# Moving the small tiles and the 2052-byte tiles of a transformer layer behind all others in SBUF

## The chip, the cores and the metric

The kernel runs on one core of a Trainium2 chip. The metric is the device time of one execution in microseconds (us), the median of several runs. TensorE (PE) multiplies matrices and loads their weights, VectorE (DVE), ScalarE (ACT) and GpSimd (POOL) work elementwise, SyncE (SP) issues the transfers.

## The reference

One layer of a trunk with stick-breaking attention and a SwiGLU feed-forward part, all in float32, for one sequence of 2048 tokens of width 1024, 16 heads of 64 and a feed-forward width of 2816.

```python
mod_all = einsum('bd,lde->lbe', silu(c), ada_w) + ada_b     # shift, scale, gate, twice
h = modulate(rms_norm(x, norm_g[0]), sh_m, sc_m)
q, k, v = split(h @ w_qkv)
sp = where(mask, softplus(z), 0)                            # z = q k / 8, mask: s < t
a = exp(where(mask, z - reverse_cumsum(sp), -inf))
y = (a @ v) @ w_o
x = x + gt_m * rms_norm(y, norm_g[1])
h = modulate(rms_norm(x, norm_g[2]), sh_f, sc_f)
y = (silu(h @ w_g) * (h @ w_u)) @ w_out
x = x + gt_f * rms_norm(y, norm_g[3])
```

## The kernel before

Every float32 product is made of three matmuls (`mm3`, L148 to L150) of a high and a low half of each operand: high by high, high by low, low by high. A matmul has 128 rows of weights (128x128) and as a rule 512 columns of the moving operand. The instructions of TensorE, ScalarE, VectorE and GpSimd are issued in the order in which the program writes them.

The work comes in these parts, by the names of their tiles:

- The attention loop, to about 1400 us. A slot of the loop handles one 128x512 block of scores: `z` (L507, two matmuls, weights `qt`, moving `kt`), two sigmoids (ScalarE, L524 and L526), a scan (VectorE, L536 or L541, into `w`), a product (GpSimd, L548, into `a`), transposes of `a` (L558, four for a block in full, moving the identity in `begin`, into `t`), a split of the transposed tile into `aT` (L568 ScalarE, L574 VectorE), and the product with the values (`o`, L586, two matmuls, weights `v`, moving `aT`). A list written out by hand, `ORDER_IN_SLOT`, sets the order in a slot: in every second slot two tiles are transposed. Between them stand the matmuls of the projections (`pj`, moving `ht`, weights `w` in tag whl) that make the queries, keys and values of later blocks.
- The output projection (`y`, weights `ohl`, moving `wo`), with transposes `h2T` (L899) between its matmuls, to about 1580 us.
- The up projection of the feed-forward part (`s`, weights `l`, moving `r`), to about 2450 us: 44 groups of 7 products with 4 steps each, 84 matmuls a group. Both factors are made by seven products instead of eight.
- The down projection (`o`, moving `b`, weights `ol_qt` and `ol_aT`): 56 accumulations of 11 steps, 8 of them with weights in `ol_qt` and 3 in `ol_aT`.

The tiles lie in one pool, `att`. A tile has a tag, a tag has as many buffers as `BUFS` says, and the pool places the tags one behind the other in the order in which they are first used. What counts below is where a tile begins in its partition, modulo 512 bytes (its residue; a weight slice of 128 float32 is 512 bytes, a moving row of 512 is 2048, so the residue is the same for every slice of a tile). The built program has them at these places:

| tags (bytes of one buffer) | what TensorE reads from them | residue before |
|---|---|---|
| `begin` (2052) | the identity for transposes, which starts 1536 bytes in | 128 |
| `ones` (512) | a few narrow sums | 160 |
| v, qt, wraw, qkn, ht, a, kt (2048 to 8192) | `v`, `qt`, `kt`, `ht`, `a`, `r` in ten of 14 steps, `l`, `b`, `ol_qt`, `ohl`, `wo` in part | 64 |
| ten, four and four tiles of 4 bytes (`rms_ssq`, `rms_ms`, `rms_rstd`) | nothing | |
| w (3 of 2052) | a few early tiles | 128, 160, 192 |
| whl (8192) | weights of the projections, `r` in the last four of 14 steps, `wo` in part | 224 |
| `sc` (32) | nothing | |
| tmp, aT (2048, 4096) | `aT`, `ol_aT`, values before their transposes | 256 |
| 18 tiles of 4 bytes (`carry`, `rms_ms2`) | nothing | |

A tile of 4 bytes takes up 32, one of 2052 takes up 2080. The steps of `r` go by `RIGHT_TAGS`:

```python
RIGHT_TAGS = [
    ("kt", "kt"), ("kt", "v"), ("v", "v"), ("qt",), ("qt",), ("qt",),
    ("kt", "kt"), ("kt", "kt"), ("v", "v"), ("v", "v"),
    ("whl",), ("whl",), ("whl",), ("whl",),
]
```

Each of the 14 serves two steps, six matmuls, so a group has 60 matmuls with `r` at 64 and then 24 with `r` at 224. In the output projection, `wo_load` puts three of the first half's four pairs in whl and all others in ht.

Of the kernel before, what the change touches and what calls it, by code (L numbers as in the profile page):

```python
# [76 lines left out]

def f32(ap):
    return ap.bitcast(F32)
# [3 lines left out]
def hybrid_trunk_kernel(  # L83
# [25 lines left out]
    ones = const.tile([P, P], F32, name="ones")  # L109
    nc.vector.memset(ones, 1.0)  # L110
# [7 lines left out]
    gc = const.tile([P, 2, KC], F32, name="gc")  # L118
    gate_rows = dram.tile([2, P, D], F32, name="gate_rows")
# [16 lines left out]
    def rms_scale(pool, src, tag, junk):  # L136

        ssq = pool.tile([P, 1], F32, name=f"{tag}_ssq", tag="rms_ssq", bufs=10)
        nc.scalar.activation(junk, src, AF.Square, accum_out=ssq)
        ms = pool.tile([P, 1], F32, name=f"{tag}_ms", tag="rms_ms", bufs=4)  # L140
        nc.vector.tensor_scalar(ms, ssq, 1.0 / D, EPS, op0=ALU.mult, op1=ALU.add)
        rstd = pool.tile([P, 1], F32, name=f"{tag}_rstd", tag="rms_rstd", bufs=4)
        nc.gpsimd.tensor_tensor(rstd, ms, mhalf, op=ALU.pow)
        return rstd
# [8 lines left out]
    att = ctx.enter_context(tc.tile_pool(name="att", bufs=2))  # L153
    zps = ctx.enter_context(tc.tile_pool(name="zps", bufs=3, space=PSUM))
# [7 lines left out]

    weights, keys, values, queries = {}, {}, {}, {}
# [3 lines left out]
    def load_weights(p, t, tag="wraw"):  # L167
        raw = att.tile([P, KC, P], F32, name=f"wr{p}_{t}", tag=tag, bufs=BUFS[tag])
        nc.sync.dma_start(raw, wqkv[p, t])
        raws[p, t] = raw  # L170

    def split_weights(p, t):
        raw = raws.pop((p, t))
        hl = att.tile([P, 2, KC, P], F32R, name=f"w{p}_{t}", tag="whl", bufs=BUFS["whl"])
        nc.scalar.copy(hl[:, 0], raw)
        nc.gpsimd.tensor_tensor(hl[:, 1], raw, f32(hl[:, 0]), op=ALU.subtract)
        weights[p, t] = hl[:, 0], hl[:, 1]

    def split_early(p, t, tags):

        raw = raws.pop((p, t))
        if len(tags) == 1:
            hl = att.tile([P, 2, KC, P], F32R, name=f"w{p}_{t}", tag=tags[0], bufs=BUFS[tags[0]])
            hi, lo = hl[:, 0], hl[:, 1]
        else:
            hi, lo = [
                att.tile([P, KC, P], F32R, name=f"w{p}_{t}_{j}", tag=tag, bufs=BUFS[tag])
# [7 lines left out]
    def ada_load(seg, half, k0, n, tag, bufs):  # L195
        w = att.tile([P, n, BT], F32, name=f"aw{seg}_{half}_{k0}", tag=tag, bufs=bufs)
        nc.sync.dma_start(w, ada_w[seg - 2, half, :, k0 : k0 + n])
        return w
# [19 lines left out]
    def ada_done(seg, ps, which, ks=slice(0, KC)):  # L218
# [6 lines left out]
        sc = att.tile([P, KC], F32, name=f"sc{which}_{ks.start}", tag="sc", bufs=1)[:, ks]  # L225
# [5 lines left out]
    def late_modulation(segs, tag, n, ahead, waits, pool, ptag, acc_tag="tmp", rows_tag="wraw", settle=3, pace=1):  # L231
# [10 lines left out]
        for at, (seg, half, k0) in enumerate(chunks):  # L242
# [5 lines left out]
            if k0 == 0:  # L248
                acc = att.tile([P, BT], F32, name=f"aacc{seg}_{half}", tag=acc_tag, bufs=BUFS[acc_tag])
# [11 lines left out]
            if seg in (2, 5):  # L261
                g = seg // 3
                rows = att.tile([P, 2, BT], F32, name=f"gr{g}_{half}", tag=rows_tag, bufs=BUFS[rows_tag])
# [17 lines left out]
    def x_load(b):  # L281
        for i in range(4):
            r0 = b * BT + i * P
            xt = att.tile([P, D], F32, name=f"x{b}_{i}", tag="v", bufs=BUFS["v"])
# [3 lines left out]
    def x_square(b, i):  # L288
        xn = att.tile([P, D], F32, name=f"xn{b}_{i}", tag="kt", bufs=BUFS["kt"])
        x_norm[b, i] = xn  # L290
        x_rstd[b, i] = rms_scale(att, x_tiles[b, i], f"n0_{b}_{i}", junk=xn)
# [16 lines left out]
    def modulate(hl, pt, which, k, name, how="aap"):  # L308

        full = att.tile([P, BT], F32, name=name, tag="tmp", bufs=BUFS["tmp"])  # L310
# [12 lines left out]
    def h_load(p, b):  # L323
        h = []
        for k2 in range(KC // 2):
            ht = att.tile([P, 2, 2, BT], F32R, name=f"ht{p}_{b}_{k2}", tag="ht", bufs=BUFS["ht"])
# [6 lines left out]
    def first_norm(b, k):  # L333
        if b is None or k >= KC:
            return
        if k % 2 == 0:
            ht = att.tile([P, 2, 2, BT], F32R, name=f"ht0_{b}_{k // 2}", tag="ht", bufs=BUFS["ht"])
# [8 lines left out]
    def unpark():  # L346
        p, b = PARKED
        kt = att.tile([P, 2, BT], F32R, name=f"kt{p}_{b}", tag="kt", bufs=BUFS["kt"])
# [5 lines left out]
        qt = att.tile([P, 2, 2, BT], F32R, name=f"qt{p}_{b}", tag="qt", bufs=BUFS["qt"])  # L354
# [5 lines left out]
        v = att.tile([P, 4, 2, 2, HD], F32R, name=f"v{p}_{b}", tag="v", bufs=BUFS["v"])  # L360
# [3 lines left out]
    def project(at):  # L364
# [43 lines left out]
        def split(acc, tag):  # L408
            hl = att.tile([P, 2, BT], F32R, name=f"{tag}n{p}_{b}", tag="qkn", bufs=BUFS["qkn"])
# [13 lines left out]
        else:  # L423
            kt = att.tile([P, 2, BT], F32R, name=f"kt{p}_{b}", tag="kt", bufs=BUFS["kt"])
# [12 lines left out]
        else:  # L437
            qt = att.tile([P, 2, 2, BT], F32R, name=f"qt{p}_{b}", tag="qt", bufs=BUFS["qt"])
# [9 lines left out]
        vT = att.tile([P, BT], F32, name=f"vT{p}_{b}", tag=tag, bufs=BUFS[tag])  # L448
        nc.scalar.copy(vT, acc)

        def values_turn():
# [6 lines left out]
            v = att.tile([P, 4, 2, 2, HD], F32R, name=f"v{p}_{b}", tag="v", bufs=BUFS["v"])  # L458
# [54 lines left out]
    def sigmoids(i, r):  # L513
# [4 lines left out]
        rest = att.tile([P, BT + 1], F32, name=f"w{i}_{r}", tag="w", bufs=BUFS["w"])  # L518
        a = att.tile([P, BT], F32, name=f"a{i}_{r}", tag="a", bufs=BUFS["a"])
# [9 lines left out]
    def break_sticks(i, r):  # L529
# [15 lines left out]
        if sc > 0:  # L545
            carries[r] = att.tile([P, 1], F32, name=f"c{i}_{r}", tag="carry", bufs=10)
# [16 lines left out]
    def split_high(i, j):  # L563
# [3 lines left out]
        hl = att.tile([P, 2, BT], F32R, name=f"aT{i}_{j}", tag="aT", bufs=BUFS["aT"])  # L567
# [10 lines left out]
    def weigh_values(i, j):  # L578
# [11 lines left out]
        if sc == 0 and j == 3:  # L590
            o = att.tile([P, BT], F32, name=f"os{p}_{e}_{qb}", tag="tmp", bufs=BUFS["tmp"])
# [12 lines left out]
    def ada_chunk(q, kh):  # L604
        ks = range(KC // 2 * kh, KC // 2 * (kh + 1))
        if q == 2:
            for k in ks:
                w = att.tile([P, 2, AQ], F32, name=f"ac{q}_{k}", tag="a", bufs=BUFS["a"])
# [4 lines left out]
        w = att.tile([P, 2, KC // 2, AQ], F32, name=f"ac{q}_{kh}", tag=tag, bufs=BUFS[tag])  # L613
# [8 lines left out]
    def ada_sum(q, k):  # L622
        w, scale = chunks[q, k], c_act[:, k : k + 1]
        if q not in piece_sums:
            acc = att.tile([P, 2, AQ], F32, name=f"asum{q}", tag="w", bufs=BUFS["w"])
# [26 lines left out]
    def ada_cols_done(q):  # L652
# [3 lines left out]
        sc = att.tile([P, KC], F32, name=f"sc0_{q}", tag="sc", bufs=1)[:, :2]  # L656
# [9 lines left out]
    def weights_high(t):  # L666
        hl = att.tile([P, 2, KC, P], F32R, name=f"w0_{t}", tag="whl", bufs=BUFS["whl"])
# [15 lines left out]
    def full_high(m):  # L683
        if m % 2 == 0:
            ht = att.tile([P, 2, 2, BT], F32R, name=f"ht0_0_{m // 2}", tag="ht", bufs=BUFS["ht"])
            first_h.extend([ht[:, 0], ht[:, 1]])
            norm_tile[0] = ht
        full = att.tile([P, BT], F32, name=f"hf0_{m}", tag="tmp", bufs=BUFS["tmp"])
# [138 lines left out]
    def mean_square(ssq, tag):  # L827

        ms = att.tile([P, 1], F32, name=f"{tag}_ms", tag="rms_ms", bufs=4)
        nc.vector.tensor_scalar(ms, ssq[0], 1.0 / D, EPS, op0=ALU.mult, op1=ALU.add)  # L830
        ms2 = att.tile([P, 1], F32, name=f"{tag}_ms2", tag="rms_ms2", bufs=4)
        nc.vector.scalar_tensor_tensor(ms2, ssq[1], 1.0 / D, ms, op0=ALU.mult, op1=ALU.add)
        rstd = att.tile([P, 1], F32, name=f"{tag}_rstd", tag="rms_rstd", bufs=4)
# [3 lines left out]
    def sum_squares(src, tag):  # L837
        junk = att.tile([P, BT], F32, name=f"{tag}_junk", tag="tmp", bufs=BUFS["tmp"])
        ssq = att.tile([P, 1], F32, name=f"{tag}_ssq", tag="rms_ssq", bufs=10)
# [6 lines left out]
    def x1_load(b, i):  # L846
        r0 = b * BT + i * P
        xt = att.tile([P, D], F32, name=f"xr{b}_{i}", tag="aT", bufs=BUFS["aT"])
# [3 lines left out]
    def y_square(b, i, half):  # L852
        acc = y_ps.pop((b, i, half))
        y_ssq[b, i, half] = sum_squares(acc, f"y{b}_{i}_{half}")
        if (b, half) == (0, 0):

            if i % 2 == 0:
                y_held[i] = att.tile([P, 2, BT], F32, name=f"yh{i}", tag="wraw", bufs=BUFS["wraw"])
            t = y_held[i - i % 2][:, i % 2]
            nc.vector.tensor_copy(t, acc)  # L860
        else:
            t = att.tile([P, BT], F32, name=f"yt{b}_{i}_{half}", tag="a", bufs=BUFS["a"])
# [25 lines left out]
    def x1_scale(b, i):  # L888
        rstd, x1 = y_rstd.pop((b, i)), x1_tiles.pop((b, i))
        for half, sl in enumerate(HALVES):  # L890
            n = att.tile([P, BT], F32, name=f"x1n{b}_{i}_{half}", tag="a", bufs=BUFS["a"])
# [3 lines left out]
    def h2_turn(b, k):  # L895
# [6 lines left out]
        full = att.tile([P, BT], F32, name=f"h2f{b}_{k}", tag="tmp", bufs=BUFS["tmp"])  # L902
# [7 lines left out]
    def o_load(b, k):  # L910
        tag = "qt" if b else "wraw"
        parts = att.tile([P, 2, BT], F32, name=f"op{b}_{k}", tag=tag, bufs=BUFS[tag])
# [5 lines left out]
    def o_add(b, k):  # L918
        parts = o_parts.pop((b, k))
        o = att.tile([P, BT], F32, name=f"of{b}_{k}", tag="tmp", bufs=BUFS["tmp"])  # L920
# [4 lines left out]
    def o_prep(b, k):  # L925
        o = o_sum.pop((b, k))
        tag = O_TAGS[b % 2][k]
        hl = att.tile([P, 2, BT], F32R, name=f"ohl{b}_{k}", tag=tag, bufs=BUFS[tag])
# [6 lines left out]
    def split_wo():  # L935

        for half, sl in enumerate(HALVES):
            for k in range(KC):
                raw = att.tile([P, BT], F32, name=f"wor{half}_{k}", tag="tmp", bufs=BUFS["tmp"])
# [3 lines left out]
                hl = att.tile([P, 2, BT], F32R, name=f"wos{half}_{k}", tag="qkn", bufs=BUFS["qkn"])  # L943
# [6 lines left out]
    def wo_load(half, k2, tag):  # L950
        hl = att.tile([P, 2, 2, BT], F32R, name=f"wo{half}_{k2}", tag=tag, bufs=BUFS[tag])
# [14 lines left out]
    def gate_load(which, tiles):  # L966
        for half, sl in enumerate(HALVES):
            tiles.append(att.tile([P, BT], F32, name=f"gate{which}_{half}", tag="w", bufs=BUFS["w"]))
# [140 lines left out]
    def sums_load(s, kt):  # L1109

        if s == 0:
            tag = "qt" if kt < 3 else "whl"
            t = att.tile([P, 4, BT], F32, name=f"ts{s}_{kt}", tag=tag, bufs=BUFS[tag])
# [8 lines left out]
        for j in range(2):  # L1122
            t = att.tile([P, 2, BT], F32, name=f"ts{s}_{kt}_{j}", tag="aT", bufs=BUFS["aT"])
# [24 lines left out]
    def right_alloc(s, m):  # L1148
        tags = RIGHT_TAGS[m]
        if len(tags) == 2:  # L1150
            right_parts[s, m] = [
                att.tile([P, 2, BT], F32R, name=f"r{s}_{m}_{j}", tag=t, bufs=BUFS[t])
                for j, t in enumerate(tags)
            ]
        else:
            t = att.tile([P, 2, 2, BT], F32R, name=f"r{s}_{m}", tag=tags[0], bufs=BUFS[tags[0]])
# [22 lines left out]
    def left_load(n):  # L1179
        for t, tag in enumerate(("wraw", "qkn")):  # L1180
            raw = att.tile([P, KC, P], F32, name=f"wi{n}_{t}", tag=tag, bufs=BUFS[tag])
# [3 lines left out]
    def left_add(n, product):  # L1185
# [9 lines left out]
        t = att.tile([P, H4, P], F32, name=f"ls{n}_{product}", tag="tmp", bufs=BUFS["tmp"])  # L1195
# [3 lines left out]
    def left_split(n, product):  # L1199
# [3 lines left out]
        if j == 0:  # L1203
            tag = "whl" if (n, pair) == (0, 0) else "ht"
            left_pair[n, pair] = att.tile(
# [25 lines left out]
    def a_load(m):  # L1231
# [3 lines left out]
            att.tile([P, 2, n, P], F32R, name=f"ol{m}_{t}", tag=t, bufs=BUFS[t])  # L1235
# [15 lines left out]
    def b_load(at, g, which):  # L1251
        par, half = block(which)
        raw = att.tile([P, BT], F32, name=f"br{at}_{g}", tag="a", bufs=BUFS["a"])
# [3 lines left out]
    def chain_tile(version, g):  # L1257

        if g < 8 and g % 2 == 0:
            tag = ("wraw", "qkn")[g // 2 % 2]  # L1260
            t = att.tile([P, 2, BT], F32, name=f"ch{version}_{g}", tag=tag, bufs=BUFS[tag])
            chain[g], chain[g + 1] = t[:, 0], t[:, 1]
        elif g >= 8:
            chain[g] = att.tile([P, BT], F32, name=f"ch{version}_{g}", tag="tmp", bufs=BUFS["tmp"])
# [12 lines left out]
    def b_split(at, g):  # L1277
        src = out_raw.pop((at, g)) if OUT_PRODUCTS[at] in (1, 2) else chain[g]
        tag = "kt" if (at * GO + g) % 14 < 7 else "v"
        hl = att.tile([P, 2, BT], F32R, name=f"b{at}_{g}", tag=tag, bufs=BUFS[tag])  # L1280
# [13 lines left out]
    def keep(src, name, tag):  # L1294
        t = att.tile([P, BT], F32, name=name, tag=tag, bufs=BUFS[tag])
# [296 lines left out]
```

## Time and profile before

| | |
|---|---|
| median of 3 runs | 2877.15 us (2875.82 to 2877.48) |
| profiled execution | 2873.52 us, of which the span of its instructions 2871.1 us |
| TensorE matmuls | 13848, busy 98% of the span |
| VectorE, ScalarE, GpSimd busy | 71%, 57%, 45% |
| transfers | 516.84 MB, mean 180 GB/s |

A row of the timeline gives the start and the drawn length of an instruction, its engine, line, operation and tiles. Matmuls overlap: the drawn length of one reaches into the next, and it is the distance of the starts that says how long TensorE spends on each.

### The profile page before, as it was taken

The page shows a single profiled execution, that of the slowest core. Times are in us where ns is not written, and L with a number is a line of the kernel's source. Part 1 is how long each engine was busy: PE and PEld are TensorE (multiplying, and loading weights), DVE is VectorE, ACT ScalarE, POOL GpSimd, SP SyncE. Part 2 cuts the span into 40 slices and gives each one's busy share as a digit, 9 for nine tenths or more (in the row PEclk, how much of TensorE's full clock was granted, in tenths as well). Part 3 has the DMA queues.
Part 4 walks back from the last instruction along what each step waited for, and adds up shares of the span by engine and source line. Part 5 has one row for each costly group of instructions (what it writes and reads, how often), then busy time and mean ns, then how long its engine had stood idle before and what let it go on. Part 6 is the DMA issues. An engine that isn't in the chain of part 4 may idle for free.

```text
span 2871.1 us, 41790 instructions
## 1 busy us (share of the span) xinstructions
PE 2818.2 (98%) x13848; PEld 2335.4 (81%) x13848; DVE 2027.7 (71%) x2821; ACT 1634.5 (57%) x3265; POOL 1280.4 (45%) x2032
## 2 busy tenths in 40 slices
PE   7999999999999999999999999999999999999998
PEld 6788888888888888887888788888778888888887
DVE  6788888888888888888866666555776655134377
ACT  5787777787777877778645533334433333322243
POOL 1465666576576655666410122221222222544454
PEclk9999999999999999999999999999999999999999
DMA  8765546656665635546389544334453335545575
GB/s 324 270 210 165 187 156 223 209 174 227 191 210 184 216 113 175 191 133 227 97 292 313 193 136 151 121 92 163 130 165 118 111 93 175 190 132 153 181 226 186
DMA packets 239367, 516.84 MB, mean 180 GB/s; under 512 B 22320, under 2 KB 110384, under 8 KB 221488
## 3 DMA queue, kind: packets, MB, share of 16 engines
q1 hardware_dynamic: 239152, 514.18, 55.2%
q8 instruction: 109, 1.79, 0.3%
q14 instruction: 106, 0.87, 0.1%
HBM read 346.85 MB, written 118.49 MB: 162 GB/s over the span
## 4 chain that ended last, share of the span: by engine, by line
PE 88%; DVE 5%; DMA 3%; ACT 2%; issue 1%; POOL 0%; SPq 0%; DVEq 0%; POOLq 0%; ACTq 0%
PE s L148 9%; PE s L149 9%; PE s L150 9%; PE o L586 8%; PE z L507 8%; PE t L558 8%; PE pj L148 6%; PE pj L149 6%; PE pj L150 6%; PE o L149 5%; PE o L148 5%; PE o L150 4%; PE y L148 1%; PE y L150 1%; PE y L149 1%
## 5 line engine op out<-in xcount | busy, mean ns | idle before, releaser
L548 POOL TENSOR_TENSOR a<-a,w 128x512 f32<-128x512 f32 (+3 forms) x640 | 620.5, 969 | 221.7 <-DVE w L541 131.7
L541 DVE TENSOR_TENSOR_SCAN w<-z,c,begin 128x512 f32<-128x512 f32 x384 | 489.8, 1279 | 87.1 <-ACT z L526 68.3
L148 PE MATMUL s<-r,l 128*128 128x512 f32 x1232 | 484.5, 393 | 7.0 <-DVE p L1352 4.5
L149 PE MATMUL s<-r,l 128*128 128x512 f32 x1232 | 482.0, 391 | 0.0
L150 PE MATMUL s<-r,l 128*128 128x512 f32 x1232 | 481.8, 391 | 0.0
L524 ACT ACTIVATE a<-z 128x512 f32<-128x512 f32 (+3 forms) x640 | 347.5, 543 | 171.8 <-PE z L507 140.8
L586 PE MATMUL o<-aT,v 128*128 128x512 f32 (+3 forms) x1280 | 387.5, 384 | 0.1
L574 DVE TENSOR_TENSOR aT<-t,aT 128x512 fp32r<-128x512 f32 (+3 forms) x640 | 359.4, 595 | 23.7 <-ACT aT L568 23.2
L507 PE MATMUL z<-kt,qt 128*128 128x512 f32 (+3 forms) x1280 | 363.5, 365 | 0.0
L568 ACT CAST aT<-t 128x512 fp32r<-128x512 f32 (+3 forms) x640 | 314.2, 534 | 75.7 <-PE t L558 65.5
L526 ACT ACTIVATE z<-z 128x512 f32<-128x512 f32 (+3 forms) x640 | 345.1, 539 | 0.0
L1360 POOL TENSOR_TENSOR one<-p,p 128x512 f32<-128x512 f32 x44 | 71.1, 1616 | 595.3 <-issue 307.6
L148 PE MATMUL pj<-ht,w 128*128 128x512 f32 x768 | 312.7, 407 | 7.6 <-ACT ht L693 2.6
L149 PE MATMUL pj<-ht,w 128*128 128x512 f32 x768 | 305.3, 398 | 1.2 <-DVE ht L698 0.7
L558 PEld LDWEIGHTS t<-begin,a 128*128 128x128 f32 x2176 | 255.7, 141 | 58.5 <-DVE aT L574 10.3
L150 PE MATMUL pj<-ht,w 128*128 128x512 f32 x768 | 302.8, 394 | 0.0
L558 PE MATMUL t<-begin,a 128*128 128x128 f32 x2176 | 294.7, 273 | 7.9 <-DVE aT L574 6.8
L148 PEld LDWEIGHTS s<-r,l 128*128 128x128 f32 x1232 | 231.5, 188 | 60.2 <-DVE p L1352 6.3
L150 PEld LDWEIGHTS s<-r,l 128*128 128x128 f32 x1232 | 231.5, 188 | 50.8
L149 PEld LDWEIGHTS s<-r,l 128*128 128x128 f32 x1232 | 231.6, 188 | 50.2 <-issue 0.5
L507 PEld LDWEIGHTS z<-kt,qt 128*128 128x128 f32 x1280 | 230.5, 188 | 40.1
L536 DVE TENSOR_TENSOR_SCAN w<-z,begin 128x128 f32<-128x128 f32 (+3 forms) x256 | 208.7, 818 | 76.4 <-ACT z L526 66.6
(159 smaller groups left out, 4868.1 us busy)
## 6 DMA issues: line engine op xcount, KB each, us to landing
ht<-h_s SPq DMA_DIRECT2D x108, 1024.0 KB, 8.2
wi<-in_win SPq DMA_DIRECT2D x86, 512.0 KB, 4.1
qt<-qn SPq DMA_DIRECT2D x124, 256.0 KB, 4.7
ol_qt<-act_s SPq DMA_DIRECT2D x56, 512.0 KB, 3.7
act_s<-S SPq DMA_DIRECT2D x66, 256.0 KB, 4.2
br<-in_wout SPq DMA_DIRECT2D x66, 256.0 KB, 3.5
h_s<-ht SPq DMA_DIRECT2D x16, 1024.0 KB, 7.8
o_s<-os SPq DMA_DIRECT2D x128, 128.0 KB, 2.4
```

The source lines that it names most:

```text
L148: nc.tensor.matmul(acc, lhs[0], rhs[0], start=first, stop=False, **kw)
L149: nc.tensor.matmul(acc, lhs[0], rhs[1], start=False, stop=False, **kw)
L150: nc.tensor.matmul(acc, lhs[1], rhs[0], start=False, stop=last, **kw)
L507: nc.tensor.matmul(z[:, :n], q[:, e, part, r * P : (r + 1) * P], k[:, e, :n], start=part == 0, stop=part == 1,)
L524: nc.scalar.activation(a[:, :n], z[:, :n], AF.Sigmoid, scale=QK_SCALE)
L526: nc.scalar.activation(z[:, :n], z[:, :n], AF.Sigmoid, scale=-QK_SCALE)
L541: nc.vector.tensor_tensor_scan(rest[:, rev], left[:, rev], begin[:, :BT][:, rev], initial=carries[r], op0=ALU.mult, op1=ALU.bypass,)
L548: nc.gpsimd.tensor_tensor(a[:, :n], a[:, :n], rest[:, 1 : n + 1], op=ALU.mult)
L558: nc.tensor.transpose(pt[:, rb * P : (rb + 1) * P], weighed[i, rb][:, j * P : (j + 1) * P], ident)
L568: nc.scalar.copy(hl[:, 0, t0:], pt[:, t0:])
L574: nc.vector.tensor_tensor(hl[:, 1, t0:], pt[:, t0:], f32(hl[:, 0, t0:]), op=ALU.subtract)
L586: nc.tensor.matmul(acc[:, t0:], lhs, hl[:, part, t0:], start=sc == qb and j == 0 and part == 0, stop=sc == 0 and j == 3 and part == 1,)
```

## The change

A second pool, `odd`, is opened behind `att` in SBUF, and the tags whose buffers are not whole multiples of 512 bytes go there. All other tiles stay in `att`, in the same order. `ones` moves behind the other constants, and a tile `fill` of 64 bytes is put behind it; it is filled once and read by nothing. All else in the program stays, instruction by instruction, but for the places in SBUF.

```diff
+ODD_TAGS = ("rms_ssq", "rms_ms", "rms_ms2", "rms_rstd", "carry", "sc", "w")
...
-    ones = const.tile([P, P], F32, name="ones")
-    nc.vector.memset(ones, 1.0)
     mhalf = const.tile([P, 1], F32, name="mhalf")
     nc.vector.memset(mhalf, -0.5)
...
     gc = const.tile([P, 2, KC], F32, name="gc")
+
+    ones = const.tile([P, P], F32, name="ones")
+    nc.vector.memset(ones, 1.0)
+    fill = const.tile([P, 16], F32, name="fill")
+    nc.vector.memset(fill, 0.0)
...
     att = ctx.enter_context(tc.tile_pool(name="att", bufs=2))
+    odd = ctx.enter_context(tc.tile_pool(name="odd", bufs=1))
...
+    def sb(shape, dtype, **kw):
+        return (odd if kw["tag"] in ODD_TAGS else att).tile(shape, dtype, **kw)
...
-        raw = att.tile([P, KC, P], F32, name=f"wr{p}_{t}", tag=tag, bufs=BUFS[tag])
+        raw = sb([P, KC, P], F32, name=f"wr{p}_{t}", tag=tag, bufs=BUFS[tag])
```

The last pair of lines stands for all others: each `att.tile` becomes `sb`. The places afterwards:

| tags | residue after |
|---|---|
| `begin` | 128 |
| `ones` | 64 |
| v, qt, wraw, qkn, ht, a, kt, whl, tmp, aT | 128 |
| w | 192, 224, 256 |

More of the change, by code (lines that the diff above doesn't have):

```diff
@@ L224, in ada_done @@
             return
-        sc = att.tile([P, KC], F32, name=f"sc{which}_{ks.start}", tag="sc", bufs=1)[:, ks]
+        sc = sb([P, KC], F32, name=f"sc{which}_{ks.start}", tag="sc", bufs=1)[:, ks]
         nc.vector.tensor_tensor(sc, ps, b_cols[:, 2 * which + 1, ks], op=ALU.add)
@@ L901, in h2_turn @@
             )
-        full = att.tile([P, BT], F32, name=f"h2f{b}_{k}", tag="tmp", bufs=BUFS["tmp"])
+        full = sb([P, BT], F32, name=f"h2f{b}_{k}", tag="tmp", bufs=BUFS["tmp"])
         nc.scalar.activation(
```

142 lines of the change are left out of this document (71 added, 71 removed).

## The prediction

> **What bounds the kernel now.** I read the page's busy times first, then the chain of waits, then the timeline of TensorE, because the first two say that nothing else needs to be read for the end of this kernel.
>
> ```profile
> PE 2818.2 (98%) x13848; PEld 2335.4 (81%) x13848; DVE 2027.7 (71%) x2821; ACT 1634.5 (57%) x3265; POOL 1280.4 (45%) x2032
> PEclk9999999999999999999999999999999999999999
> PE 88%; DVE 5%; DMA 3%; ACT 2%; issue 1%; POOL 0%; SPq 0%; DVEq 0%; POOLq 0%; ACTq 0%
> ```
>
> TensorE is busy for 98% of the span at full clock, and 88% of the chain that ended last is TensorE's own work, so what it spends on each matmul is the kernel's time. The busy column can't give that price: each 128x512 matmul is drawn about 390 ns long and overlaps the next one. The distance from one start to the next is the price. It can be read off the timeline of TensorE (columns: start in us, drawn length, engine, line, operation, tiles, count), between two rows whose number of matmuls in between is known.
>
> The first stretch lies in the up projection of the feed-forward part (tile `s`). A group there is 84 matmuls of 512 columns: 60 whose moving tile `r` has the tags kt, v and qt, at residue 64, then 24 whose `r` has the tag whl, at residue 224. The weights `l` are at 64 in all of them. At 1697.91 the 60 end and the 24 begin.
>
> ```profile
> 1690.43 0.39 PE L148 MATMUL s<-r,l 128*128 128x512 f32 x1
> ...
> 1697.91 0.40 PE L148 MATMUL s<-r,l 128*128 128x512 f32 x1
> ...
> 1703.53 0.40 PE L148 MATMUL s<-r,l 128*128 128x512 f32 x1
> ```
>
> Same line, same engines beside it, same weights: 33 matmuls in 7.48 us are 226.7 ns each, and the next 24 in 5.62 us are 234.2 ns each. What changed is the residue of the moving tile. That difference, 7.5 ns, is the subject of this prediction.
>
> The second stretch is in the down projection (tile `o` with `b`): nine matmuls whose weights `ol_aT` are at 256 from 2500.17 on, then fifteen whose weights `ol_qt` are at 64 from 2502.23 on, all with the moving tile at 64.
>
> ```profile
> 2500.17 0.39 PE L148 MATMUL o<-b,ol_aT 128*128 128x512 f32 x1
> ...
> 2502.23 0.39 PE L148 MATMUL o<-b,ol_qt 128*128 128x512 f32 x1
> ...
> 2505.63 0.39 PE L148 MATMUL o<-b,ol_qt 128*128 128x512 f32 x1
> ```
>
> 2.06 us over 9 are 228.9 ns, 3.40 us over 15 are 226.7 ns. So it matters on the weights' side too, and the cheap value returns when both operands stand at one residue.
>
> The third stretch is the attention loop, which mixes projections `pj` (moving ht at 64, weights whl at 224), scores `z` (64 and 64), value products `o` (moving aT at 256, weights 64) and transposes `t` (moving begin at 128, weights `a` at 64).
>
> ```profile
> 712.79 1.04 PE L558 MATMUL t<-begin,a 128*128 128x128 f32 x8
> 713.59 0.70 PE L586 MATMUL o<-aT,v 128*128 128x512 f32 x2
> 714.13 0.62 PE L507 MATMUL z<-kt,qt 128*128 128x512 f32 x2
> ...
> 717.63 0.60 PE L558 MATMUL t<-begin,a 128*128 128x128 f32 x4
> ```
>
> From 714.13 to 717.63 there are 15 matmuls of 512 columns (four z, two o, nine pj): 233.3 ns each, 6.6 above the cheap value, and the z among them pay although both their operands are at 64. The order of the stream matters, then, not only the matmul itself.
>
> The fourth stretch shows how long. In the output projection (tile `y`) four transposes at 128 and 64 are followed by matmuls with both operands at 64: once nine, once twenty-four.
>
> ```profile
> 1453.80 0.40 PE L149 MATMUL y<-wo,ohl 128*128 128x512 f32 x1
> ...
> 1455.67 0.60 PE L899 MATMUL h2T<-begin,x1n 128*128 128x128 f32 x4
> ...
> 1466.49 0.39 PE L149 MATMUL y<-wo,ohl 128*128 128x512 f32 x1
> ...
> 1467.88 0.39 PE L149 MATMUL y<-wo,ohl 128*128 128x512 f32 x1
> ...
> 1471.73 0.40 PE L148 MATMUL y<-wo,ohl 128*128 128x512 f32 x1
> ```
>
> The first eight of the nine (after the one that directly follows the transposes) take 1.87 us, 233.8 ns each. Of the twenty-four, six take 1.39 us (231.7 ns each), and the next 17 take 3.85 us (226.5 ns each). A stream at one residue thus falls into the cheap step, but only after some six matmuls, and something at another residue throws it out again.
>
> **The change part by part.** It moves addresses. The order of the instructions on all five engines, their shapes and what they wait for stay as they are, but for three fills on VectorE. Afterwards every large tile that TensorE reads is at 128, and so is the identity in `begin`; only `w` (a few early reads) and `ones` (a few narrow matmuls) are elsewhere. How many matmuls each class has is read from the groups by line and shape:
>
> ```profile
> L148 PE MATMUL s<-r,l 128*128 128x512 f32 x1232 | 484.5, 393 | 7.0 <-DVE p L1352 4.5 <-ACT p L1296 2.4
> L148 PE MATMUL pj<-ht,w 128*128 128x512 f32 x768 | 312.7, 407 | 7.6 <-ACT ht L693 2.6 <-DVE qn L411 1.4 <-issue 1.4
> L586 PE MATMUL o<-aT,v 128*128 128x512 f32 x896 | 302.0, 418 | 0.1
> L558 PE MATMUL t<-begin,a 128*128 128x128 f32 x2176 | 294.7, 273 | 7.9 <-DVE aT L574 6.8 <-POOL w L176 0.5
> L507 PE MATMUL z<-kt,qt 128*128 128x512 f32 x896 | 282.5, 396 | 0.0
> L148 PE MATMUL y<-wo,ohl 128*128 128x512 f32 x256 | 104.0, 406 | 0.0
> L149 PE MATMUL o<-b,ol_aT 128*128 128x512 f32 x168 | 66.2, 394 | 0.0
> L148 PE MATMUL o<-b,ol_qt 128*128 128x512 f32 x448 | 174.3, 389 | 0.0
> ...
> L574 DVE TENSOR_TENSOR aT<-t,aT 128x512 fp32r<-128x512 f32 (+3 forms) x640 | 359.4, 595 | 23.7 <-ACT aT L568 23.2
> ```
>
> *Up projection.* 3 x 1232 = 3696 matmuls, 24 in 84 of them at 224: 1056. They lose 7.5 ns each: 7.9 us. No transposes come between, so I take this whole.
>
> *Down projection.* 3 x 168 = 504 matmuls with `ol_aT`, 2.2 ns each: 1.1 us.
>
> *Attention loop.* 3 x 768 pj, 896 z and 896 o make 4096 matmuls of 512 columns. Those directly behind transposes (713.59 to 714.13 holds two o in 0.54 us, so one of them is longer for another reason) and those that wait for another engine I leave out, one in nine: 3640 are left. At 6.6 ns each there are 24.0 us to be had if the cheap step holds always. But transposes still come, and I can't see from this trace whether eight transposes at 128 and 128 keep the step. I take it that they don't, and that six matmuls behind each run of them still pay 5.0 ns (231.7 less 226.7). L574 splits each turned tile once, so there are 640 of them; the order written out for a slot puts two in a run, which makes 320 runs with 4096 / 320 = 12.8 matmuls each, one of which directly follows. Six of 11.8 paying 5.0 of 6.6 ns keep 39% of the loss; 61% of 24.0 us is 14.6 us.
>
> *Output projection.* 3 x 256 = 768 matmuls. Three of the eight weight tiles have the tag whl, so 288 matmuls have the moving tile at 224, and at some 7 ns they are worth 2.0 us. Transposes come between in part of it, so I take 1.3; the bounds are 0.5 and 2.8 (a further 0.8 for the nine at 1453.80 and their like).
>
> *Transposes.* 2176 in the loop, and some 400 elsewhere. In the run at 712.79, eight reach to the next start in 0.80 us, a little over 0.1 us each. No row has a transpose with both operands at one residue. The nearest rows are those of the `s` stretch, where equal residues take 3% off a step; I bound a transpose by the same 3% either way, 3.3 ns, which over 2176 is plus or minus 7 us. I take zero, because no row gives the sign.
>
> *The fills.* `ones` moves behind `mhalf`, and a fill of 128x16 is new.
>
> ```profile
> 0.83 0.17 DVE L110 MEMSET ones<- 128x128 f32 x1 [0.83 <-PEq L1579]
> 0.95 0.06 DVE L112 MEMSET mhalf<- 128x1 f32 x1
> 1.01 0.06 DVE L620 MEMSET acol<- 128x4 f32 x1
> 6.45 0.15 DVE L141 TENSOR_SCALAR n_ms<-n_ssq 128x1 f32<-128x1 f32 x1 [5.38 <-ACT xn L139]
> ```
>
> VectorE then sits idle for 5.38 us, which hides 0.06 to 0.17 us; without that cover it would cost just that.
>
> *The other engines.* Their tiles move too. The scan that writes `w` has three buffers at three residues (128, 160, 192) already:
>
> ```profile
> L541 DVE TENSOR_TENSOR_SCAN w<-z,c,begin x384: 1251/1282/1286, 122.1 to 1403.9; 128x512 f32<-128x512 f32 x192
> ```
>
> Shortest, median and longest lie within 3%, so VectorE does not care; I take zero for it, ScalarE and GpSimd.
>
> *What is late next.* In the middle of the attention loop:
>
> ```profile
> 400.00:1200.00 800.00, 792.56 (x4340) 667.26 (x4338) 684.07 (x891) 626.15 (x1318) 509.55 (x1046) 1.00 0.58 189
> ```
>
> The columns after the length are TensorE, its weight loads, VectorE, ScalarE and GpSimd. VectorE is busy 684 of 800 us. If TensorE's part shrinks by 2%, VectorE goes from 86% to 87%; it stays behind, but some waits grow (the transposes wait 6.8 us in all for aT, above). I bound what is given back between nothing and a fifth of the loop's 14.6 us, 2.9, and take 1.5.
>
> Sum: 7.9 + 1.1 + 14.6 + 1.3 - 1.5 = 23.4 us. The profiled execution took 2873.5 us, 3.6 below the median of 2877.15; a saving of this kind is the same in each, so 2877.15 - 23.4 = 2853.8 us (2850.1 for an execution like the profiled one).
>
> A rule speaks against the change. The Trainium skill, "TensorE: Matmul & The Clock Gate", section "Step-by-step: what each phase is for", says that TensorE has two independent read ports and that "Loading the next tile's weights doesn't steal SBUF read bandwidth from the running matmul". By that rule where the two operands lie would not matter and the sum would be zero; the 226.7 against 234.2 ns above, in one line, disagree.
>
> **The rivals.** *The step holds through the transposes too.* Then the whole 24.0 us of the loop come, and 2.0 of the output projection: 7.9 + 1.1 + 24.0 + 2.0, less a tenth of the loop's, 2.4, given back, is 32.6: 2844.5 us. For it: all tiles then have one distance. Against: the step of a transpose isn't that of a matmul, and order mattered even among matmuls at 64.
>
> *Transposes throw it out for good.* For it: the nine at 1453.80 never settled. The loop then keeps all its loss and only 7.9 + 1.1 + 0.5 = 9.5 us come: 2867.7 us.
>
> *Nothing moves.* The slower step would come from something else that the whl tiles have, such as being written by GpSimd or read in another order; 2877 us. Against: in the `s` stretch r is loaded by the same queue and written by ScalarE and VectorE whatever its tag. The rule quoted above would also give this time.
>
> *Slower: the cheap step belongs to residue 64, not to equality.* Every equal pair in this trace stands at 64, none at 128. If a tile at 128 pays what one at 224 pays, those now cheap go from 226.7 to 234.2: 2640 `s`, 1344 of the down projection with `ol_qt` (its groups have 448 in each of three lines) and some 480 `y`, 4464 x 7.5 = 33 us, against nothing gained: 2910 us. It decides in the `s` stretch: above 230 ns per matmul with r in kt, it is this. For it: no row excludes it. Against: with weights at 256 and the moving tile at 64, the price is 228.9, neither 226.7 nor 234.2, so it goes with the pair.
>
> **How the numbers follow.** The forecast has 0.50, the step that holds throughout 0.21, the loop that keeps its loss 0.14, nothing 0.06, slower 0.09. The first three are faster by over 0.2% (5.8 us, about what a measurement of this kernel can tell from no change): 0.85; the same 0.06; slower 0.09. The predicted time is the likeliest, 2853.8 us. The range leaves out the slower case and no change, and about a twentieth beyond the gains. Below, it reaches past 2844.5 by most of the transposes' 7 us: 2838. Above, it takes in 2867.7 and a little of their cost: 2870.
>
> **What would show it.** In the profile after: the `s` stretch at 226.7 ns through all 84 matmuls of a group; the nine `ol_aT` at 226.7; in the attention loop, matmuls that fall from 233 to 226.7 some way behind each run of transposes, or all at once; transposes still at 0.11 us; waits of TensorE in the loop a little longer. I am wrong if an `s` with r in kt takes over 230 ns, if the loop's 233 ns stays, or if VectorE's scan takes more than its 1282 ns.

## The result, and the profile after

| | before | changed |
|---|---|---|
| median of 6 runs each | 2875.9 us (2871.06 to 2877.48) | 2856.2 us (2853.0 to 2860.04) |
| profiled execution | 2873.52 us | 2853.0 us |
| its span | 2871.1 us | 2851.0 us |

The ratio of the times is 0.9933, with a 95% interval of 0.992 to 0.9946: faster by 19.7 us in the median and by 20.1 in the span of the two profiled executions. The prediction said 23.4. The changed kernel's page, in the lines that the prediction showed first (busy times, granted clock, shares of the chain that ended last):

```profile
PE 2798.8 (98%) x13848; PEld 2336.3 (82%) x13848; DVE 2021.7 (71%) x2822; ACT 1631.8 (57%) x3265; POOL 1276.4 (45%) x2032
PEclk9999999999999999999999999999999999999999
PE 87%; DVE 5%; ACT 3%; issue 2%; DMA 2%; POOL 1%; SPq 0%; DVEq 0%; POOLq 0%; ACTq 0%
```

TensorE has as many matmuls as before and the same share of a shorter span; its idle time went from 2871.1 - 2818.2 = 52.9 to 2851.0 - 2798.8 = 52.2 us. So the 20 us came out of what a matmul costs, and not out of waits. The timeline of TensorE says where. Line numbers are 7 higher in `mm3`, now L155 to L157, and 12 higher in what follows it.

The up projection, one group of 84 matmuls: its start, its 61st matmul (the first with `r` in whl) and the 85th.

```profile
1956.94 0.39 PE L155 MATMUL s<-r,l 128*128 128x512 f32 x1
...
1970.54 0.39 PE L155 MATMUL s<-r,l 128*128 128x512 f32 x1
...
1975.98 0.39 PE L155 MATMUL s<-r,l 128*128 128x512 f32 x1
```

60 in 13.60 us are 226.7 ns each, and the 24 with `r` in whl take 5.44 us, 226.7 ns each, where they took 234.2 before. The down projection, with weights in `ol_qt` from 2482.71 and in `ol_aT` from 2488.15 on:

```profile
2482.71 0.39 PE L155 MATMUL o<-b,ol_qt 128*128 128x512 f32 x1
...
2488.15 0.39 PE L155 MATMUL o<-b,ol_aT 128*128 128x512 f32 x1
...
2489.96 0.39 PE L157 MATMUL o<-b,ol_aT 128*128 128x512 f32 x1
```

24 in 5.44 us are 226.7 ns each, and the eight steps behind `ol_aT` take 1.81, 226.3 each (228.9 before). The attention loop, behind a run of eight transposes:

```profile
712.87 1.03 PE L570 MATMUL t<-begin,a 128*128 128x128 f32 x8
713.66 0.71 PE L598 MATMUL o<-aT,v 128*128 128x512 f32 x2
714.21 0.62 PE L519 MATMUL z<-kt,qt 128*128 128x512 f32 x2
714.66 0.39 PE L155 MATMUL pj<-ht,w 128*128 128x512 f32 x1
...
716.02 0.62 PE L598 MATMUL o<-aT,v 128*128 128x512 f32 x2
716.48 0.33 PE L519 MATMUL z<-kt,qt 128*128 128x128 f32 x2
```

From 714.21 to 716.48 are ten matmuls in 2.27 us, 227.0 ns each; the same kind of stretch took 233.3 before. Behind the transposes the stream has to settle, that is, to come back to the cheap step of 226.7 ns. In the output projection, behind four transposes, that takes longer:

```profile
1453.84 0.39 PE L156 MATMUL y<-wo,ohl 128*128 128x512 f32 x1
...
1455.68 0.60 PE L911 MATMUL h2T<-begin,x1n 128*128 128x128 f32 x4
1456.04 0.48 PE L155 MATMUL y<-wo,ohl 128*128 128x512 f32 x1
1456.35 0.40 PE L156 MATMUL y<-wo,ohl 128*128 128x512 f32 x1
...
1458.44 0.39 PE L156 MATMUL y<-wo,ohl 128*128 128x512 f32 x1
...
1459.80 0.39 PE L156 MATMUL y<-wo,ohl 128*128 128x512 f32 x1
```

The first matmul behind the transposes, at 1456.04, takes 0.31 us. From 1456.35 on nine in 2.09 us are 232.2 ns each, and then six in 1.36 are 226.7. Step by step the nine take 235, 233, 236, 224, 231, 236, 228, 233 and 231 ns. The eight from 1453.84 to the transposes, which took 233.8 ns each before, take 230.0: they settle in part before the next transposes come.

These are samples. The sum over all is made from the starts of all 13848 matmuls: for each of 512 columns the step to the next start less 226.67 ns (for 384 and 256 columns less 170.0 and 113.3); steps that are over 20 ns longer are waits and are counted apart.

| excess over the cheap step, us | before | changed | gained |
|---|---|---|---|
| up projection, `s` | 8.51 | 0.57 | 7.9 |
| down projection, `ol_aT` | 1.17 | 0.00 | 1.2 |
| loop, `pj` | 13.69 | 6.67 | 7.0 |
| loop, `z` | 5.69 | 5.20 | 0.5 |
| loop, `o` | 4.72 | 2.18 | 2.5 |
| output projection, `y` | 2.83 | 1.15 | 1.7 |
| all (with `ol_qt`, about 0) | 36.60 | 15.78 | 20.8 |

### The profile page after: what moved, and what is told of

Its sections match the earlier page's. It is cut to its first block, busy times and chain, and to the rows that moved or that the text cites. A ratio compares the mean times of both kernels' runs of the same rounds, so it can differ in the third digit from the quotient of the medians.

```text
span 2851.0 us, 41791 instructions
## 1 busy us (share of the span) xinstructions
PE 2798.8 (98%) x13848; PEld 2336.3 (82%) x13848; DVE 2021.7 (71%) x2822; ACT 1631.8 (57%) x3265; POOL 1276.4 (45%) x2032
## 4 chain that ended last, share of the span: by engine, by line
PE 87%; DVE 5%; ACT 3%; issue 2%; DMA 2%; POOL 1%; SPq 0%; DVEq 0%; POOLq 0%; ACTq 0%
PE s L155 9%; PE s L157 9%; PE s L156 9%; PE z L519 8%; PE o L598 8%; PE t L570 8%; PE pj L155 6%; PE pj L156 6%; PE pj L157 6%; PE o L157 4%; PE o L156 4%; PE o L155 4%; PE y L157 2%; PE y L155 2%; PE y L156 2%
## 5 line engine op out<-in xcount | busy, mean ns | idle before, releaser
L155 PE MATMUL s<-r,l 128*128 128x512 f32 x1232 | 482.9, 392 | 5.9 <-DVE p L1364 3.5
L157 PE MATMUL s<-r,l 128*128 128x512 f32 x1232 | 480.5, 390 | 0.0
L155 PE MATMUL pj<-ht,w 128*128 128x512 f32 x768 | 310.0, 404 | 7.6 <-ACT ht L705 2.6
L157 PE MATMUL pj<-ht,w 128*128 128x512 f32 x768 | 302.5, 394 | 0.0
L155 PEld LDWEIGHTS s<-r,l 128*128 128x128 f32 x1232 | 231.7, 188 | 56.7 <-DVE p L1364 5.2
L157 PEld LDWEIGHTS s<-r,l 128*128 128x128 f32 x1232 | 231.8, 188 | 48.4
L156 PEld LDWEIGHTS s<-r,l 128*128 128x128 f32 x1232 | 231.8, 188 | 48.1 <-issue 0.5
```

The costliest lines, as they stand in the source:

```text
L155: nc.tensor.matmul(acc, lhs[0], rhs[0], start=first, stop=False, **kw)
L156: nc.tensor.matmul(acc, lhs[0], rhs[1], start=False, stop=False, **kw)
L157: nc.tensor.matmul(acc, lhs[1], rhs[0], start=False, stop=last, **kw)
```

## The experiments

Two things had to be told apart from what the prediction says: whether it is the *distance* between the two operands that counts (theory 1), or where a tile stands by itself, modulo 64 or 256 bytes say (theory 2); and what throws the stream out of the cheap step, the identity's place or the transposes as such. All edits are made on the changed kernel, whose tiles stand at 128. In the lists below a distance is that of the weights less that of the moving tile, modulo 256.

**All tiles 32 bytes further.** A tile of 32 bytes ahead of all others puts every residue from 128 to 160.

```diff
+    lead = const.tile([P, 8], F32, name="lead")
+    nc.vector.memset(lead, 0.0)
     begin = ...
```

> A tile of 32 bytes ahead of all others puts every tile that TensorE reads at residue 160 instead of 128, the identity too; all distances stay. If the price of a matmul goes by the distance of the two operands (theory 1), nothing changes: 2856 us, the up projection at 226.7 ns a matmul with r in any tag. If it goes by where a tile starts against lines of 64 bytes (theory 2: before, 224 was the one residue off such a line; 160 is off it too), every matmul pays some 234 ns: the up projection alone adds 3696 x 7.5 = 28 us, over all 10000 matmuls of 512 columns up to 75 us, 2884 to 2930 us.

Measured: 2856.22 us, against 2874.65 for the kernel before on the same chip; ratio 0.993 (0.9913 to 0.9946). The first and the 85th matmul of a group of the up projection:

```profile
1962.06 0.39 PE L157 MATMUL s<-r,l 128*128 128x512 f32 x1
...
1981.10 0.39 PE L157 MATMUL s<-r,l 128*128 128x512 f32 x1
```

84 in 19.04 us are 226.7 ns each, at a residue that is no multiple of 64. The excess is 15.35 us in all. The time is that of the changed kernel. The place itself does not matter, so theory 2 falls.

**The identity at another residue.** Without `fill` the large tiles stand at 64, the identity stays at 128.

```diff
-    fill = const.tile([P, 16], F32, name="fill")
-    nc.vector.memset(fill, 0.0)
```

> The changed kernel without the 64 byte fill: every large tile at 64, the identity stays at 128, so only the transposes have their operands 64 bytes apart. If the identity's place matters for how the stream falls out of the cheap step (theory 1 with transposes as part of the stream), the matmuls behind transposes change: the loop's pj, z and o pay more than in the changed kernel, up to 10 us in all. If any run of transposes throws the stream out whatever its residue, pj, z and o pay what they do in the changed kernel, some 3 to 5 ns each, and the time is 2856 us within 3. The up projection stays at 226.7 ns in both, which also says that 64 and 128 are alike.

Measured: 2859.33 us; ratio 0.9945 (0.993 to 0.996), an interval that overlaps that of the changed kernel. That is 3.1 us above the changed kernel's median, where 2856 within 3 was expected. The stretch of the loop that stands above:

```profile
713.23 1.03 PE L568 MATMUL t<-begin,a 128*128 128x128 f32 x8
714.02 0.71 PE L596 MATMUL o<-aT,v 128*128 128x512 f32 x2
714.56 0.62 PE L517 MATMUL z<-kt,qt 128*128 128x512 f32 x2
...
716.83 0.33 PE L517 MATMUL z<-kt,qt 128*128 128x128 f32 x2
```

The ten matmuls behind 714.56 take 2.27 us here too, and the excess is 15.97 us (`pj` 6.70, `z` 5.30, `o` 2.18). In steps the identity's place is worth 0.2 us, which is nothing. Its trace has 1.9 us more of waits, and the changed kernel's own runs spread from 2853.0 to 2860.04 us.

**Only whl elsewhere.** Five kernels move whl by D bytes and leave the residues of all else as they are. They stand here in the order in which they ran. A pad of D bytes stands before whl, and one of 512 - D behind it (for D of 64, 448).

```diff
+    nc.vector.memset(att.tile([P, D // 4], F32, name="pad_whl", tag="pad_whl", bufs=1), 0.0)
     weights_high(1)
...
+    nc.vector.memset(att.tile([P, (512 - D) // 4], F32, name="pad_tmp", tag="pad_tmp", bufs=1), 0.0)
     full_high(0)
```

D of 64:

> The changed kernel with the four whl buffers alone at 192, 64 bytes beyond all others. Theory 1 (distance): the 24 matmuls of a group of the up projection with r in whl cost over 226.7 ns, between 228 and 235; pj too, so 10 to 20 us slower than the changed kernel. Theory 2 (64 byte lines): nothing changes, 226.7 ns and 2856 us.

D of 256:

> The same with the whl buffers at 384, half of 512 bytes away. Theory 1: over 226.7 ns for the 24 matmuls of a group, how much tells how the price goes with the distance (229 at the 192 of ol_aT before, 234 at the 160 of whl). Theory 2: nothing changes. A third case, that only distances off 64 byte lines cost (a mixture), would also give 226.7 ns here and in the run at 64.

D of 128:

> The changed kernel with the whl buffers at 256, 128 bytes beyond all others. So far 64 bytes cost and 256 cost nothing, so the price repeats after 256 bytes or fewer. If it repeats after 128 (theory 1a), r in whl and pj cost what they do in the changed kernel, 226.7 ns and 229.3 ns. If after 256 (theory 1b), this is half a period: pj and the 24 matmuls with r in whl cost more than 229 ns, and both alike, since 128 forward and 128 back are then the same distance.

D of 32:

> The whl buffers at 160, 32 bytes beyond all others: the smallest distance that the pool can make. If the price repeats after 256 and goes by the signed distance of the weights from the moving tile, pj (weights 32 ahead) costs 230 to 234 ns and r in whl (weights 32 behind) 227 to 230. If a distance only counts from 64 bytes on, both are as in the changed kernel.

D of 160, which is as far as whl stood from the others before (224 less 64):

> The other part of the change undone: the whl buffers alone 160 bytes beyond all others, as far as they were before, tmp and aT with the others. r in whl goes back to 234 ns and pj to 233, ol_aT stays at 226.7. With what the runs at 32, 64 and 128 bytes cost (14 to 18 us more than the changed kernel), 2871 to 2875 us; if whl is the greater part of the change, it takes back at least three quarters of the gain of 20 us.

For each, in the order 64, 256, 128, 32 and 160, the row of the first of 24 matmuls with `r` in whl, and that of the first behind them:

```profile
1984.87 0.40 PE L155 MATMUL s<-r,l 128*128 128x512 f32 x1
...
1990.38 0.40 PE L155 MATMUL s<-r,l 128*128 128x512 f32 x1
```

```profile
1975.72 0.39 PE L155 MATMUL s<-r,l 128*128 128x512 f32 x1
...
1981.16 0.39 PE L155 MATMUL s<-r,l 128*128 128x512 f32 x1
```

```profile
1984.10 0.40 PE L155 MATMUL s<-r,l 128*128 128x512 f32 x1
...
1989.70 0.39 PE L155 MATMUL s<-r,l 128*128 128x512 f32 x1
```

```profile
1985.86 0.40 PE L155 MATMUL s<-r,l 128*128 128x512 f32 x1
...
1991.46 0.40 PE L155 MATMUL s<-r,l 128*128 128x512 f32 x1
```

```profile
1982.81 0.40 PE L155 MATMUL s<-r,l 128*128 128x512 f32 x1
...
1988.42 0.40 PE L155 MATMUL s<-r,l 128*128 128x512 f32 x1
```

| D | 24 steps, us | ns each | excess in all, us | time, us | runs |
|---|---|---|---|---|---|
| 0 (the changed kernel) | 5.44 | 226.7 | 15.78 | 2856.2 | 6 |
| 32 | 5.60 | 233.3 | 33.43 | 2873.12 | 1 |
| 64 | 5.51 | 229.6 | 30.67 | 2870.11 | 1 |
| 128 | 5.60 | 233.3 | 32.21 | 2869.98 | 1 |
| 160 | 5.61 | 233.8 | 34.11 | 2871.76 | 10 |
| 256 | 5.44 | 226.7 | 15.54 | 2859.81 | 1 |

The price has a period of 256 bytes: at 256 it is that of 0, and at 128 it is not. With D of 32 I had expected less than was measured, a price that grows with the distance; it does not grow, it is nearly whole at 32 and smaller at 64. The mean step of `pj`, whose weights lie in whl, goes from 229.8 ns in the changed kernel to 232.5, 232.7 and 232.8 with D of 32, 64 and 128.

In these 24 the moving tile lies D ahead, so the distance is -D. One class of matmuls has it the other way round, and the table of places ahead does not list it: for the first 24 matmuls of `s`, `left_split` puts the weights `l` in whl, and `r` lies in kt and v. For D of 64 the first and the 24th of them:

```profile
1578.15 0.40 PE L155 MATMUL s<-r,l 128*128 128x512 f32 x1
...
1583.52 0.39 PE L157 MATMUL s<-r,l 128*128 128x512 f32 x1
```

23 in 5.37 us are 233.5 ns each, where a distance of -64 costs 229.6. With D of 32, 128 and 160 the same 23 take 233.1, 232.8 and 233.4 ns each, and with D of 0 and 256 they take 226.7. So the sign of the distance counts at 64.

With D of 160 the gain is almost gone: ratio 0.999 (0.998 to 1.0) to the kernel before, 2871.76 against 2873.95 us on one chip. That undoes one part of the change alone, and it shows that whl is most of it: 34.11 - 15.78 = 18.3 of the 20.8 us in steps come back.

**Only aT and its like elsewhere.** One pad of 192 bytes puts tmp and aT as far from the others as before, with whl left among them.

```diff
+    nc.vector.memset(att.tile([P, 48], F32, name="pad_tmp", tag="pad_tmp", bufs=1), 0.0)
     full_high(0)
```

> One part of the change undone: tmp and aT go 192 bytes on, as far from the other tiles as they were before, whl stays with the others. The nine matmuls with ol_aT should go back to 229.0 ns (1.2 us in all), o in the loop from 2.6 to some 4 to 5 ns above 226.7, and z and pj behind it pay a little more too: 5 to 8 us slower than the changed kernel, 2861 to 2864 us. If most of the gain came from aT, not from whl, it is over 12 us.

One run gave 2857.58 us, 1.4 above the median of the changed kernel and within its runs. The same kernel, in four more runs:

> The kernel with tmp and aT alone 192 bytes on, again, for its time: the trace of its first run had 4.4 us more in the steps of TensorE than the changed kernel. 2859 to 2862 us; together with the run at 160 bytes the two parts should make up the 20 us, within 3.

Measured: 2861.62 us against 2873.95; ratio 0.9955 (0.994 to 0.9969). Its first row with `ol_aT` in an accumulation, and the row behind the nine:

```profile
2479.35 0.39 PE L155 MATMUL o<-b,ol_aT 128*128 128x512 f32 x1
...
2481.41 0.39 PE L155 MATMUL o<-b,ol_qt 128*128 128x512 f32 x1
```

Nine in 2.06 us are 228.9 ns, as before the change. In the loop, the excess of `o` is 4.94 us instead of 2.18, and that of `pj` is 7.87 instead of 6.67, though `pj` itself reads nothing there. That of `z` falls, from 5.20 to 4.28, where a little more was expected. In all it is 20.18 us, and 20.11 in the trace of the timed kernel. By steps, then, whl alone is worth 36.60 - 20.11 = 16.5 us, aT alone 36.60 - 34.11 = 2.5, and both together 20.8: the parts aren't quite independent, presumably because a matmul at another distance also throws out those that follow. By time, aT's part is not told from none: the intervals of the changed kernel and of this one overlap.

**No narrow transposes in one place.** In the output projection, the four transposes of 128 columns before `h2f` are replaced by one matmul of 512 columns with the identity as weights. This kernel leaves out the turning of the tile, so its output is not that of the layer.

```diff
+    ident_r = const.tile([P, P], F32R, name="ident_r")
+    nc.scalar.copy(ident_r, ident)
...
-        for i in range(4):
-            c0 = (k % 4) * P
-            nc.tensor.transpose(
-                pt[:, i * P : (i + 1) * P], x1_norm[b, i, k // 4][:, c0 : c0 + P], ident
-            )
+        nc.tensor.matmul(pt, ident_r, x1_norm[b, k % 4, k // 4], start=True, stop=True)
```

> The changed kernel in which the four transposes of each h2T tile are replaced by one matmul of 512 columns with the identity as weights; the tile is then not transposed, so the output differs. If the narrow transposes are what throws the stream out of its cheap step, y and h2T stay at 226.7 ns from one to the next and the 1.15 us that y pays above it fall under 0.3; the 318 ns step behind h2T goes too. If any change of tile does it, y pays about what it did. The span falls by 32 x (4 x 0.109 + 0.09 - 0.227) = 10 us in the first case and 7 in the second.

Measured: 2849.22 us in one run. Two of the replaced transposes, with the matmuls of the output projection between them:

```profile
1437.81 0.39 PE L158 MATMUL y<-wo,ohl 128*128 128x512 f32 x1
...
1439.62 0.39 PE L911 MATMUL h2T<-x1n,ident_r 128*128 128x512 f32 x1
...
1441.88 0.39 PE L911 MATMUL h2T<-x1n,ident_r 128*128 128x512 f32 x1
```

Eight in 1.81 us and then ten in 2.26 are 226 ns each: no settling, and the excess of `y` falls from 1.15 to 0.36 us (under 0.3 was expected). So another tile's matmul in between does not throw the stream out, and the transposes did. The edit changes their width and their number format together and doesn't tell which of the two does it; the matmuls of 384 columns, below, speak for the width. The time itself says little: it is one run, and four steps of 109 ns became one of 227, 32 times, 6.7 us by itself. The span fell by 3.5 us and not by the 10 expected: `s` waits for 15.3 us in this trace, and for 10.9 in the changed kernel's.

## Why the prediction was right, and where its sum was off

**The mechanism** was right: what counts is whether weights and moving tile stand at one residue. This is shown by whl moved away (most of the gain goes) and by all tiles moved together (it stays). Two things were not in the prediction: it is the residue modulo 256 bytes and not 512, and the price doesn't grow with the distance but goes by its sign and size (233.3 ns at -32, 229.6 at -64, 233.5 at 64).

**Up projection**, predicted 7.9 us: 7.9 in the steps. **Down projection**, predicted 1.1: 1.2. **Output projection**, predicted 1.3 between 0.5 and 2.8: 1.7. **Transposes**, taken as 0 between -7 and 7: 109.05 ns each before and 108.97 after, so 0, and the residue of the identity makes no difference to them. **Fills**, 0: VectorE's third fill ends at 1.05 us, and ahead of its first calculation the engine still idles for 5.22 us.

```profile
0.98 0.07 DVE L125 MEMSET fill<- 128x16 f32 x1
...
6.34 0.15 DVE L148 TENSOR_SCALAR n_ms<-n_ssq 128x1 f32<-128x1 f32 x1 [5.22 <-ACT xn L146]
```

**Other engines**, 0: the scan's shortest, median and longest time are those of before but for one of 2 ns, with its three buffers at 192, 224 and 256. The window of the loop (TensorE, weight loads, VectorE, ScalarE, GpSimd):

```profile
L553 DVE TENSOR_TENSOR_SCAN w<-z,c,begin x384: 1253/1282/1286, 121.8 to 1394.1; 128x512 f32<-128x512 f32 x192
```

```profile
400.00:1200.00 800.00, 792.24 (x4372) 672.46 (x4371) 687.86 (x896) 628.68 (x1326) 512.77 (x1056) 1.00 0.59 192
```

In 800 us TensorE does 4372 matmuls instead of 4340, 0.7% more, and VectorE is busy for 688 us instead of 684, 86% in both; the prediction had 87%.

**The loop** is the term that was mis-sized: predicted 14.6 us, measured 7.0 + 0.5 + 2.5 = 10.0. What was to be had is right: the sum of steps before is 13.69 + 5.69 + 4.72 = 24.1 us where the prediction had 24.0. What it got wrong is how much of that stays: 14.0 us instead of 9.4. It had put 6 x 5.0 = 30 ns behind each of 320 runs of transposes. The trace does have 320: 192 runs of eight, 64 of seven and 64 of three. Count for each the excess of the `pj`, `z` and `o` behind it, up to the next matmul of another kind. Where no matmul of 384 columns is among these, in 225 cases, it is 28.7 ns in the mean, near what was reckoned. Where there are some, in 95, it is 63.1 ns, and these make 6.0 of 12.4 us in all. The other 1.6 us lie elsewhere in the stage. So the step that failed is the count of what throws the stream out: the prediction took the transposes alone. One of the runs of three:

```profile
839.06 0.49 PE L570 MATMUL t<-begin,a 128*128 128x128 f32 x3
839.31 0.71 PE L598 MATMUL o<-aT,v 128*128 128x512 f32 x2
839.86 0.63 PE L519 MATMUL z<-kt,qt 128*128 128x512 f32 x2
840.32 0.40 PE L155 MATMUL pj<-ht,w 128*128 128x512 f32 x1
...
841.01 0.51 PE L598 MATMUL o<-aT,v 128*128 128x384 f32 x2
841.36 0.62 PE L519 MATMUL z<-kt,qt 128*128 128x512 f32 x2
841.82 0.40 PE L155 MATMUL pj<-ht,w 128*128 128x512 f32 x1
```

The steps from 839.31 on, in ns: 318, 231, 236, 228, 232, 232, 227 for 512 columns, 170 and 175 for the two of 384, and then 236, 228, 232, 231, 227, 226, 227. The stream had settled by 841.01, and the two matmuls of 384 columns, at one residue like all others, threw it out again. Blocks on the diagonal of the mask have narrower matmuls, so the stream settles twice there. The prediction counted matmuls of 512 columns and what lies between transposes, and took no account of those of other widths. That these throw the stream out is read from the traces: 61 of the runs of three have matmuls of 384 columns behind them and leave 67.4 ns each, the other three leave 9.0. No kernel was run without them. That 30 ns came out as the mean without them is in part luck. The prediction let six matmuls pay behind each run; in the trace some runs are followed by the cheap step at once (318, then 227, 227, 226), and others leave some 40 ns.

**Given back**, predicted 1.5 us, in the loop. In the loop nothing was: the waits and long steps of `pj` and `o` come to 49.0 us before and 48.5 after. In the feed-forward part, which the prediction had taken whole, `s` waits for 10.9 us instead of 10.3, and `o` with `b` for 1.27 instead of 0.65. That is 1.2 us of waits there. The size was near by luck, since the place was wrong. The starts of the two stages agree. Before, the first matmul of the up and of the down projection:

```profile
1579.65 0.39 PE L148 MATMUL s<-r,l 128*128 128x512 f32 x1
...
2442.22 0.40 PE L148 MATMUL o<-b,ol_qt 128*128 128x512 f32 x1
```

and after:

```profile
1567.58 0.39 PE L155 MATMUL s<-r,l 128*128 128x512 f32 x1
...
2422.87 0.39 PE L155 MATMUL o<-b,ol_qt 128*128 128x512 f32 x1
```

12.1 us are gained ahead of the up projection (predicted 14.6 + 1.3 - 1.5 = 14.4), and 19.4 - 12.1 = 7.3 in it. So the sum by its own steps is 7.9 + 1.2 + 10.0 + 1.7 - 1.2 = 19.6 us, beside 20.1 in the span.

**The rivals.** The step doesn't hold through the transposes (28.7 ns are lost in the mean behind a run, where no matmul of 384 columns follows), nor is the stream thrown out for good: the nine of the output projection, which showed no settling before, are down from 233.8 to 230.0 ns. "Nothing moves" and "the cheap step belongs to residue 64" fell with the first trace. The Trainium skill, "TensorE: Matmul & The Clock Gate", section "Step-by-step: what each phase is for", says that loading the next tile's weights takes no SBUF read bandwidth from the running matmul. The prediction had drawn from it that the places would not matter; here they are worth up to 7.5 ns of each step (226.7 against 234.2), whatever the cause in the hardware is.

**What stays open.** Whether the running matmul's own weights or those of the next one, which load meanwhile, set the price. Only a matmul at a change of weights tells these apart. The last `y` before the first `s` has its own operands in line, and the weights behind it lie in whl. It takes 227 ns in the changed kernel, 237 before the change and with D of 160, 232 and 235 with D of 128 and 32, but 226 with D of 64. In the loop a second `z` ahead of a `pj` is in the same position. In 64 places with the order o, o, z, z, pj, pj, pj, o, o, z, z, pj the last `z` takes 226.6 ns in the mean in the changed kernel, and 237.4, 231.8, 233.7 and 230.0 with D of 160, 128, 32 and 64. Both speak for the weights of the next one. But the `y` is one matmul a run and the `z` stand in a stream that is settling, so it isn't shown. Open as well is why a stream needs up to nine matmuls to settle, and what decides how many.

## What to carry to other kernels

Read the price of a matmul from start to start, in stretches of one kind: the drawn lengths (0.39 us) overlap, and neither they nor the busy share show a loss of 3% in each. Where TensorE sets the end, look at whether weights and moving tiles have the same place modulo 256 bytes in their partition: here small tiles and odd lengths went behind the large ones, for float32 matmuls of 512 columns, and the gain was 0.7%. Long runs of matmuls of one width kept the cheap step. Behind narrower ones the next matmuls lost up to some 40 ns in all, so a sum over a mixed stream must count every width.

## What the runs showed of the hardware

- A 128x512 float32 step costs 226.7 ns at equal residues modulo 256 bytes. Otherwise, by distance (weights less moving), in stretches of one kind: -64 costs 229.6 (whl moved by 64; 228.9 for `ol_aT`), 64 costs 233.5, -32 costs 233.3, 32 costs 233.1, 128 costs 232.8 to 233.3, 96 costs 233.8 to 234.2, and -96 costs 233.4.
- It repeats from 256 bytes on: 226.7 at 256 as at 0.
- VectorE's scan doesn't change over residues from 128 to 256 (1282 ns in the median), nor does a transpose (109 ns) with its identity at an equal or another residue.
- Behind something narrow, in the changed kernel, the stream runs through the end of one order of steps (233, 236, 224, 231, 236, 228, 233, 231, then 226.7 ns), with a nanosecond or two of play. It joins the order at different points: behind the four transposes at 1455.68 it goes through the whole, in the run of three at 839.06 it starts at a later 231, and behind the eight at 712.87 it has only the last two. From the third matmul behind the transposes on, all 221 stretches of six or more matmuls of 512 columns follow this order within 2.5 ns.
